# FFN's second product: one more slot of seven products, earlier first sums, and the last tile's end in column halves

## The chip, the core and the metric

The kernel runs on one core of a Trainium2 chip. The metric is the device time of one execution in microseconds (us). Five engines work side by side, each through its own instructions in order: TensorE (PE; its weight loads are PEld) multiplies, VectorE (DVE) and ScalarE (ACT) work on elements, GpSimd (POOL) does a few small things here, and SyncE (SP) issues nearly all DMA transfers.

## The reference

One decoder block for 256 tokens of width 2048 in float32: a retention branch and an attention branch, merged by gates, then a gated FFN of width 5632 with a causal convolution, and a final RMS norm. The change lies in the last lines of it:

```python
up = causal_dwconv(h2 @ w_ffn_up[l], conv_w[l], conv_b[l])
a, b = jnp.split(up, 2, axis=-1)
x = x + (jax.nn.silu(a) * b) @ w_ffn_down[l]
return rmsnorm(x, final_norm_w)
```

## The kernel before

**Products in three.** Each float32 operand is split into a first part (whi, gh, ...) and a second part, the rest (wlo, gl, ...), both of type fp32r. `split2` (line 158) makes them: ScalarE copies and rounds (line 161), VectorE subtracts (line 162). A product is three matmuls of 128x128 by 128x512, first by first, first by second, second by first (`mm3`, line 172).

**Weights.** All weights come as one stream of blocks of 128x1024. `load` brings a block into one of four `raw` buffers, `part` splits it into one of four pairs of part buffers, and when a block's splits are done, `part` issues the load of the block four places on. A slot uses two blocks. The loop of slot i issues first the splits for slot i+1, then the tasks that wait (`run_tasks`), then the matmuls of slot i; each engine's instructions keep this order.

**FFN.** The first product runs in groups of two 128-wide pieces ("up", four slots each, kc 0 to 3); its results g stay as 44 pieces, 22 blocks of two.

**The second product** (`down_slots`, line 794) is 2048 columns wide and taken in two pairs (p = 0, 1) of 512-wide columns. Each pair has 22 slots (q = 0 to 21). An ordinary slot multiplies a block of 256 rows by two columns for both token tiles: 8 products, 24 matmuls. A slot in `SEVEN` (line 82) does the same 2x2 scheme in seven products (21 matmuls), in the way of Strassen and Winograd. For it `seven_parts` (line 674) makes sums and differences of the weights, VectorE and ScalarE in turn, lines 680 to 695, in place of the two ordinary splits; and `seven_sums` (line 708) makes those of g once for each block, lines 714 to 718 and a split. The sums are used in both pairs: before, for blocks 0 to 5, made in loops q = 1, 4, 7, 10, 13 and 16 of the first pair.

**The end of the second pair.** After the last slot of seven, `gathered` (line 762) adds four extra accumulators into the residual in two halves of four VectorE operations (lines 770 to 773, 775 to 778), one in each of two loops. `added` adds the ordinary accumulators (line 783) and squares (line 787). `weighted` (line 789) multiplies by the final norm's weights wf. Slots 20 and 21 are held together: column 3 of their four blocks is computed for token tile 0 and then for tile 1, 24 matmuls each, and `finish` (line 530) ends each tile: add, squares, power on GpSimd (line 547), scale, store.

In the following, "slot n" without a pair is one of the second pair.

Of the kernel before, what the change touches and what calls it, by code (L numbers as in the profile page):

```python
# [9 lines left out]
F32 = mybir.dt.float32  # L10
# [68 lines left out]

SEVEN = ((4, 7, 10, 13, 16, 18), (3, 5, 8, 10, 13, 15))


def down():
# [16 lines left out]
def block(ctx: ExitStack, tc: tile.TileContext, a):  # L102
# [424 lines left out]
        yield  # L527
        split2(*ffn_slot(f), g)

    def finish(acc, t):  # L530

        c, half = D // CW - 1, CW // 2
        w = slice(c * CW, (c + 1) * CW)
        x3 = big["x2"][:, t, :]
        ms = sb.tile([P, 3], F32, name="r3ms", bufs=2)
        r = sb.tile([P, 1], F32, name="r3", bufs=2)
        nc.vector.reduce_sum(ms[:, 2:], big["ss3"][:, t, :c], axis=AX.X)  # L537
        nc.vector.tensor_scalar(ms[:, 0:1], ms[:, 2:], 1.0 / D, EPS, op0=OP.mult, op1=OP.add)  # L538
        pieces = [slice(c * CW + i * half, c * CW + (i + 1) * half) for i in range(2)]
        for i, v in enumerate(pieces):  # L540
            nc.vector.tensor_add(x3[:, v], acc[:, i * half:(i + 1) * half], x3[:, v])  # L541
        for i, v in enumerate(pieces):
            sq = sb.tile([P, half], F32, name="sq3", bufs=2)
            nc.scalar.activation(sq, x3[:, v], AF.Square, accum_out=big["ss3"][:, t, c + i:c + i + 1])  # L544
            nc.vector.scalar_tensor_tensor(ms[:, i + 1:i + 2], big["ss3"][:, t, c + i:c + i + 1], 1.0 / D,  # L545
                                           ms[:, i:i + 1], op0=OP.mult, op1=OP.add)
        nc.gpsimd.tensor_tensor(r, ms[:, 2:], mhalf[:, :1], op=OP.pow)  # L547
        nc.vector.tensor_mul(x3[:, w], x3[:, w], big["wf"][1][:, CW:])
        step = 448
        for b in range(0, 3 * step, step):  # L550
            w = slice(b, b + step)
            nc.vector.tensor_scalar_mul(x3[:, w], x3[:, w], r)  # L552
            nc.sync.dma_start(orows[:, t, w], x3[:, w])
        w = slice(3 * step, D)
        nc.scalar.activation(x3[:, w], x3[:, w], AF.Copy, scale=r)
        nc.scalar.dma_start(orows[:, t, w], x3[:, w])


    now = {}
# [145 lines left out]
            return ot[x + "h"][:, f % 8:f % 8 + 2, :], ot[x + "l"][:, f % 8:f % 8 + 2, :]  # L705
        return big["gh"][:, f - 16:f - 14, :], big["gl"][:, f - 16:f - 14, :]

    def seven_sums(k):


        ah, al = two_blocks(k)
        room = big["room"]
        x, sums = room[:, 0, :].rearrange("p (k t) -> p k t", k=2), room[:, 1, :].rearrange("p (i t) -> p i t", i=4)
        nc.vector.tensor_add(x, f32(ah), f32(al))
        nc.vector.tensor_add(sums[:, 0, :], x[:, 0, P:], x[:, 1, P:])
        nc.vector.tensor_sub(sums[:, 2, :], x[:, 0, :P], x[:, 0, P:])
        nc.vector.tensor_sub(sums[:, 1, :], sums[:, 0, :], x[:, 0, :P])
        nc.vector.tensor_sub(sums[:, 3, :], x[:, 1, :P], sums[:, 1, :])
        pool_k, tag = (px, f"xb{k}") if k < 5 else (big["pf"], "wa")
        big["s", k] = pool_k.tile([P, 2, 4, P], F32R, name=f"s{k}", tag=tag, bufs=1)  # L720
        split2(big["s", k][:, 0], big["s", k][:, 1], sums)

    def seven_products(k, accs, extra, halves):

        xs = two_blocks(k)
        sums = big["s", k]

        def a(t, kk):
            return [x[:, kk, t * P:(t + 1) * P] for x in xs]

        def b(half, kk):
            return [x[:, kk * CW:(kk + 1) * CW] for x in halves[half]]

        ss = [[sums[:, x, i, :] for x in range(2)] for i in range(4)]
        t1, t4 = [[x[:, i * CW:(i + 1) * CW] for x in big["t14"]] for i in range(2)]
        t2 = [big["t2"][:, x, :] for x in range(2)]
        for key, (ah, al), (bh, bl) in (
                ("e0", a(0, 0), b(0, 0)), ((0, 0), a(0, 1), b(0, 1)), ((0, 1), ss[3], b(1, 1)),
                ("e3", ss[2], b(1, 0)), ("e2", ss[1], t2), ("e1", ss[0], t1), ((1, 0), a(1, 1), t4)):
            begin, end = accs.edges(key, 3)  # L740
            mm3(accs.bank(key), ah, al, bh, bl, begin, end, to=stream)
# [52 lines left out]
    def down_slots(slot):  # L794
# [4 lines left out]
        for i, (seven, where) in enumerate(slots):  # L799
# [13 lines left out]
            if i + 1 < len(slots):  # L813
                if slots[i + 1][0]:
                    seven_parts(n)
                else:
                    part(n)
                    part(n + 1)
            if p == 0 and q in (1,) + SEVEN[0][:-1]:
                seven_sums(((1,) + SEVEN[0]).index(q))  # L820
            if q == SEVEN[p][-1] + 1:
                spawn(gathered, at)
            if p == 1 and q == SEVEN[1][-1] + 1:
                big["wf"] = [big["pf"].tile([P, 2 * CW], F32, name="wf", tag=x, bufs=1) for x in ("wa", "wb")]
                for j, wf in enumerate(big["wf"]):
                    nc.sync.dma_start(wf, a["wf"][None, 2 * CW * j:2 * CW * (j + 1)].to_broadcast([P, 2 * CW]))
            if p == 1 and q == per - 4:
                spawn(added, at.main[1], 3, False)
            if p == 1 and q == per - 3:
                weighted(0, 2)  # L830
            if p == 1 and q == per - 2:
                spawn(added, at.main[0], 2)
# [7 lines left out]
            elif p == 1 and q >= per - 2:  # L840
                if q == per - 2:
                    held = list(zip(where, halves))
                else:
                    held += zip(where, halves)
                    for t in range(NT):
                        acc = at.extra[t][:, 0, :]
                        for h, ((k, d), (hi, lo)) in enumerate(held):
                            for j in range(2):
                                x = [y[:, j, t * P:(t + 1) * P] for y in two_blocks(k)]
                                w = slice(j * CW, (j + 1) * CW)  # L850
                                mm3(acc, *x, hi[:, w], lo[:, w], h + j == 0, h == 3 and j == 1, to=stream)
                        issue()
                        finish(acc, t)
            else:
                for (k, d), (hi, lo) in zip(where, halves):
                    xs = two_blocks(k)
                    for j in range(2):
                        w = slice(j * CW, (j + 1) * CW)
                        for t in range(NT):
                            key = (t, d - 2 * p)  # L860
                            begin, end = at.edges(key, 3)
                            mm3(at.bank(key), *(x[:, j, t * P:(t + 1) * P] for x in xs), hi[:, w], lo[:, w],
                                begin, end, to=stream)
                issue()
# [29 lines left out]
    for kind, n, _, _, rows in groups:  # L894
# [10 lines left out]
        for kc in range(nk // 4):  # L905
            for h in range(2):
                part_x(4 * slot + 4 + 2 * h)
                part(2 * slot + 2 + h)
            run_tasks()
            halves = [parts.pop(2 * slot + h) for h in range(2)]  # L910
            products(kind, n, act, accs, kc, halves, range(NT), nk)
# [2 lines left out]
        closed(kind, n, acc, more)  # L914
    big["t14"] = [px.tile([P, 2 * CW], F32R, name=f"t14{i}", tag=f"xb{5 + i}", bufs=1) for i in range(2)]
    big["t2"] = px.tile([P, 2, CW], F32R, name="t2", tag="xb7", bufs=1)
    big["room"] = big["pf"].tile([P, 2, CW], F32, name="room", tag="wb", bufs=1)
    down_slots(slot)
    assert not tasks and not between
    right.close()  # L920
# [71 lines left out]
```

## Time and profile before

| what | us |
|---|---|
| median of three runs | 1432.77 (1432.64 to 1432.97) |
| the profiled execution | 1433.07 |
| its span, first to last instruction | 1431.3 |
| TensorE busy in the span | 1420.4 |
| VectorE busy | 977.1 |
| ScalarE busy | 743.4 |

The busy time of TensorE counts matmuls that overlap in its pipeline, so single matmuls last longer (0.39) than the distance of their starts. Times in rows are us from the first instruction.

### The profile page before, as it was taken

How to read it: one execution, taken by the hardware profiler on the slowest of the kernel's cores; microseconds unless marked ns; L12 is line 12 of the kernel's file. 1: busy time of each engine (PE TensorE's matmuls, PEld its weight loads, DVE VectorE, ACT ScalarE, POOL GpSimd, SP SyncE). 2: the span in 40 equal slices, each digit the busy share in tenths (PEclk: the TensorE clock that was granted, in tenths of full speed). 3: DMA queues.
4: the chain of work that ended last, by engine and by line, in shares of the span. 5: the costliest groups of instructions: out<-in, count | busy, mean ns of one | idle time of the engine just before them, and what ended most of it. 6: DMA issues, size and time to landing. Idle time of an engine off the chain costs nothing. (4 is left out here: it accounts for less than half of the span.)

```text
span 1431.3 us, 19149 instructions
## 1 busy us (share of the span) xinstructions
PE 1420.4 (99%) x7290; PEld 1214.8 (85%) x7290; DVE 977.1 (68%) x1296; ACT 743.4 (52%) x1006; POOL 6.0 (0%) x14
## 2 busy tenths in 40 slices
PE   9999999999999999999999999999999999999997
PEld 7888888888888888888888888888888888888886
DVE  6687656657554545455567777777777778898787
ACT  6545454544544444444465555555555555555553
POOL 0000000000000000000000000000000000000000
PEclk9999999999999999999999999999999999999999
DMA  8755565555566666666656666565665655656664
GB/s 295 263 181 163 163 190 167 189 175 189 180 186 196 187 195 186 195 214 200 195 188 189 194 182 197 182 195 188 188 194 181 199 181 168 198 192 206 206 215 167
DMA packets 77836, 276.22 MB, mean 193 GB/s; under 512 B 8720, under 2 KB 10288, under 8 KB 77744
## 3 DMA queue, kind: packets, MB, share of 16 engines
q1 hardware_dynamic: 77312, 274.27, 60.3%
q8 instruction: 57, 0.93, 0.3%
q10 hardware_dynamic: 432, 0.73, 0.1%
q14 instruction: 35, 0.29, 0.1%
HBM read 272.86 MB, written 2.10 MB: 192 GB/s over the span
## 5 line engine op out<-in xcount | busy, mean ns | idle before, releaser
L162 DVE TENSOR_TENSOR wlo<-raw,whi 128x1024 fp32r<-128x1024 f32 (+1 forms) x481 | 573.3, 1219 | 373.9 <-ACT whi L161 239.4
L161 ACT ACTIVATE whi<-raw 128x1024 fp32r<-128x1024 f32 (+1 forms) x481 | 502.2, 1056 | 513.7 <-PE acc L170 372.8
L170 PE MATMUL acc<-xb,whi 128*128 128x512 f32 x1920 | 466.2, 392 | 1.2 <-ACT whi L161 1.2
L170 PEld LDWEIGHTS acc<-xb,whi 128*128 128x128 f32 x1920 | 350.7, 188 | 68.8 <-ACT whi L161 2.3
L170 PE MATMUL acc<-whi,xb 128*128 128x512 f32 x896 | 282.1, 391 | 0.0
L170 PEld LDWEIGHTS acc<-xb,wlo 128*128 128x128 f32 x1920 | 250.8, 191 | 12.3
L170 PE MATMUL acc<-xb,wlo 128*128 128x256 f32 x1920 | 254.6, 282 | 0.0
L170 PEld LDWEIGHTS acc<-whi,xb 128*128 128x128 f32 x896 | 168.3, 188 | 34.4
L170 PE MATMUL acc<-wlo,xb 128*128 128x512 f32 x448 | 174.6, 390 | 0.0
L170 PEld LDWEIGHTS acc<-wlo,xb 128*128 128x128 f32 x448 | 84.2, 188 | 16.7
L170 PE MATMUL acc<-wlo,gh 128*128 128x512 f32 x224 | 87.4, 390 | 0.2 <-DVE wlo L162 0.2
L170 PE MATMUL acc<-whi,gl 128*128 128x512 f32 x224 | 87.2, 389 | 0.0
L170 PE MATMUL acc<-whi,gh 128*128 128x512 f32 x224 | 87.1, 389 | 0.0
L521 DVE SCALAR_TENSOR_TENSOR y<-u,vec,y 128x256 f32<-128x256 f32 x176 | 73.5, 480 | 0.0
L170 PEld LDWEIGHTS acc<-wlo,gh 128*128 128x128 f32 x224 | 42.0, 188 | 9.7 <-DVE wlo L162 1.0
L170 PE MATMUL acc<-whi,mgh 128*128 128x512 f32 x128 | 50.1, 392 | 0.0
L170 PE MATMUL acc<-whi,mgl 128*128 128x512 f32 x128 | 49.8, 389 | 0.0
L170 PE MATMUL acc<-wlo,mgh 128*128 128x512 f32 x128 | 49.8, 389 | 0.0
L170 PEld LDWEIGHTS acc<-whi,gh 128*128 128x128 f32 x224 | 42.0, 188 | 8.8
L170 PEld LDWEIGHTS acc<-whi,gl 128*128 128x128 f32 x224 | 42.0, 188 | 8.7
L518 ACT ACTIVATE y<-u,vec 128x256 f32<-128x256 f32 x88 | 47.6, 588 | 0.0
L170 PE MATMUL acc<-whi,otmh 128*128 128x512 f32 x104 | 40.6, 390 | 0.0
(206 smaller groups left out, 1167.9 us busy)
## 6 DMA issues: line engine op xcount, KB each, us to landing
raw<-in_wts SPq DMA_DIRECT2D x503, 512.0 KB, 4.0
rows<-in_x SPq DMA_DIRECT2D x4, 512.0 KB, 6.9
xp<-in_x SPq DMA_DIRECT2D x4, 512.0 KB, 5.2
xt<-in_xT SPq DMA_DIRECT2D x3, 512.0 KB, 7.2
out<-x SPq DMA_DIRECT2D x6, 224.0 KB, 2.9
wf<-in_wf SPq DMA_DIRECT2D x2, 512.0 KB, 7.2
out<-x ACTq DMA_DIRECT2D x2, 352.0 KB, 3.1
xt<-in_xT SPq DMA_DIRECT2D x2, 256.0 KB, 4.5
```

Of the source, the lines that this page charges most:

```text
L161: nc.scalar.activation(hi, full, AF.Copy)
L162: nc.vector.tensor_sub(lo, full, f32(hi))
L170: to.append(lambda: nc.tensor.matmul(out, a, b, **kw))
L518: nc.scalar.activation(y[:, j, :], u[:, j, 0:S], AF.Identity, scale=cv[j][:, 0:1], bias=cv[j][:, 3:4])
L521: nc.vector.scalar_tensor_tensor(y[:, j, :], u[:, j, i:i + S], cv[j][:, i:i + 1], y[:, j, :], op0=OP.mult, op1=OP.add)
```

## The change

- `SEVEN` gets a seventh slot in the second pair, 17; the sums of block 6 that it needs are made in loop 6 of that pair, into the room of two buffers of the FFN.
- The sums of block 0 are made in the FFN's last group (n = 42, kc = 1) and not in loop 1 of the first pair. They take the room where the sums of block 5 were, and those another.
- As `gathered` starts after the last slot of seven, its halves move from loops 16 and 17 to loops 18 and 19. The wf transfers are issued in loop 8 instead of 16, the first two columns are weighted in loop 11 instead of 19.
- The second token tile: its last block's products go into a second accumulator, in two halves of 256 columns; `finish` adds the first accumulator for the whole column and then half by half.
- `finish` writes the results in three transfers instead of four, 512, 1024 and 512 columns; the last column's multiplication by wf goes into its scaling.

```diff
--- before.py
+++ after.py
@@ -79,7 +79,7 @@
 
 
 
-SEVEN = ((4, 7, 10, 13, 16, 18), (3, 5, 8, 10, 13, 15))
+SEVEN = ((4, 7, 10, 13, 16, 18), (3, 5, 8, 10, 13, 15, 17))
 
 
 def down():
@@ -527,7 +527,7 @@
         yield
         split2(*ffn_slot(f), g)
 
-    def finish(acc, t):
+    def finish(acc, t, more):
 
         c, half = D // CW - 1, CW // 2
         w = slice(c * CW, (c + 1) * CW)
@@ -536,24 +536,30 @@
         r = sb.tile([P, 1], F32, name="r3", bufs=2)
         nc.vector.reduce_sum(ms[:, 2:], big["ss3"][:, t, :c], axis=AX.X)
         nc.vector.tensor_scalar(ms[:, 0:1], ms[:, 2:], 1.0 / D, EPS, op0=OP.mult, op1=OP.add)
+        if more is not None:
+            nc.vector.tensor_add(x3[:, w], acc, x3[:, w])
+            acc = more
         pieces = [slice(c * CW + i * half, c * CW + (i + 1) * half) for i in range(2)]
         for i, v in enumerate(pieces):
             nc.vector.tensor_add(x3[:, v], acc[:, i * half:(i + 1) * half], x3[:, v])
-        for i, v in enumerate(pieces):
             sq = sb.tile([P, half], F32, name="sq3", bufs=2)
             nc.scalar.activation(sq, x3[:, v], AF.Square, accum_out=big["ss3"][:, t, c + i:c + i + 1])
+        for i in range(2):
             nc.vector.scalar_tensor_tensor(ms[:, i + 1:i + 2], big["ss3"][:, t, c + i:c + i + 1], 1.0 / D,
                                            ms[:, i:i + 1], op0=OP.mult, op1=OP.add)
         nc.gpsimd.tensor_tensor(r, ms[:, 2:], mhalf[:, :1], op=OP.pow)
-        nc.vector.tensor_mul(x3[:, w], x3[:, w], big["wf"][1][:, CW:])
-        step = 448
-        for b in range(0, 3 * step, step):
+        step = CW
+        for b in range(0, D, step):
             w = slice(b, b + step)
-            nc.vector.tensor_scalar_mul(x3[:, w], x3[:, w], r)
-            nc.sync.dma_start(orows[:, t, w], x3[:, w])
-        w = slice(3 * step, D)
-        nc.scalar.activation(x3[:, w], x3[:, w], AF.Copy, scale=r)
-        nc.scalar.dma_start(orows[:, t, w], x3[:, w])
+            if b == step:
+                nc.scalar.activation(x3[:, b:b + 2 * step], x3[:, b:b + 2 * step], AF.Copy, scale=r)
+                nc.scalar.dma_start(orows[:, t, b:b + 2 * step], x3[:, b:b + 2 * step])
+            elif b == 0:
+                nc.vector.tensor_scalar_mul(x3[:, w], x3[:, w], r)
+                nc.sync.dma_start(orows[:, t, w], x3[:, w])
+            elif b == 3 * step:
+                nc.vector.scalar_tensor_tensor(x3[:, w], x3[:, w], r, big["wf"][1][:, CW:], op0=OP.mult, op1=OP.mult)
+                nc.sync.dma_start(orows[:, t, w], x3[:, w])
 
 
     now = {}
@@ -705,7 +711,7 @@
             return ot[x + "h"][:, f % 8:f % 8 + 2, :], ot[x + "l"][:, f % 8:f % 8 + 2, :]
         return big["gh"][:, f - 16:f - 14, :], big["gl"][:, f - 16:f - 14, :]
 
-    def seven_sums(k):
+    def seven_sums(k, pool_k, tag):
 
 
         ah, al = two_blocks(k)
@@ -716,9 +722,12 @@
         nc.vector.tensor_sub(sums[:, 2, :], x[:, 0, :P], x[:, 0, P:])
         nc.vector.tensor_sub(sums[:, 1, :], sums[:, 0, :], x[:, 0, :P])
         nc.vector.tensor_sub(sums[:, 3, :], x[:, 1, :P], sums[:, 1, :])
-        pool_k, tag = (px, f"xb{k}") if k < 5 else (big["pf"], "wa")
-        big["s", k] = pool_k.tile([P, 2, 4, P], F32R, name=f"s{k}", tag=tag, bufs=1)
-        split2(big["s", k][:, 0], big["s", k][:, 1], sums)
+        if isinstance(tag, str):
+            both = pool_k.tile([P, 2, 4, P], F32R, name=f"s{k}", tag=tag, bufs=1)
+            big["s", k] = both[:, 0], both[:, 1]
+        else:
+            big["s", k] = [pool_k.tile([P, 4, P], F32R, name=f"s{k}" + x, tag=x, bufs=1) for x in tag]
+        split2(*big["s", k], sums)
 
     def seven_products(k, accs, extra, halves):
 
@@ -731,7 +740,7 @@
         def b(half, kk):
             return [x[:, kk * CW:(kk + 1) * CW] for x in halves[half]]
 
-        ss = [[sums[:, x, i, :] for x in range(2)] for i in range(4)]
+        ss = [[x[:, i, :] for x in sums] for i in range(4)]
         t1, t4 = [[x[:, i * CW:(i + 1) * CW] for x in big["t14"]] for i in range(2)]
         t2 = [big["t2"][:, x, :] for x in range(2)]
         for key, (ah, al), (bh, bl) in (
@@ -816,17 +825,20 @@
                 else:
                     part(n)
                     part(n + 1)
-            if p == 0 and q in (1,) + SEVEN[0][:-1]:
-                seven_sums(((1,) + SEVEN[0]).index(q))
+            if p == 0 and q in SEVEN[0][:-1]:
+                k = SEVEN[0].index(q) + 1
+                seven_sums(k, px, f"xb{k % 5}")
+            if p == 1 and q == 6:
+                seven_sums(6, big["pf"], ("u0", "u1"))
             if q == SEVEN[p][-1] + 1:
                 spawn(gathered, at)
-            if p == 1 and q == SEVEN[1][-1] + 1:
+            if p == 1 and q == 8:
                 big["wf"] = [big["pf"].tile([P, 2 * CW], F32, name="wf", tag=x, bufs=1) for x in ("wa", "wb")]
                 for j, wf in enumerate(big["wf"]):
                     nc.sync.dma_start(wf, a["wf"][None, 2 * CW * j:2 * CW * (j + 1)].to_broadcast([P, 2 * CW]))
             if p == 1 and q == per - 4:
                 spawn(added, at.main[1], 3, False)
-            if p == 1 and q == per - 3:
+            if p == 1 and q == 11:
                 weighted(0, 2)
             if p == 1 and q == per - 2:
                 spawn(added, at.main[0], 2)
@@ -843,14 +855,20 @@
                 else:
                     held += zip(where, halves)
                     for t in range(NT):
-                        acc = at.extra[t][:, 0, :]
+                        acc, more = (at.extra[t][:, i, :] for i in range(2))
                         for h, ((k, d), (hi, lo)) in enumerate(held):
                             for j in range(2):
                                 x = [y[:, j, t * P:(t + 1) * P] for y in two_blocks(k)]
-                                w = slice(j * CW, (j + 1) * CW)
-                                mm3(acc, *x, hi[:, w], lo[:, w], h + j == 0, h == 3 and j == 1, to=stream)
+                                if t == 0 or h < 3:
+                                    w = slice(j * CW, (j + 1) * CW)
+                                    mm3(acc, *x, hi[:, w], lo[:, w], h + j == 0, h == 3 - t and j == 1, to=stream)
+                        for b in range(0, CW, CW // 2) if t else ():
+                            for j in range(2):
+                                x = [y[:, j, t * P:(t + 1) * P] for y in two_blocks(k)]
+                                w = slice(j * CW + b, j * CW + b + CW // 2)
+                                mm3(more[:, b:b + CW // 2], *x, hi[:, w], lo[:, w], j == 0, j == 1, to=stream)
                         issue()
-                        finish(acc, t)
+                        finish(acc, t, more if t else None)
             else:
                 for (k, d), (hi, lo) in zip(where, halves):
                     xs = two_blocks(k)
@@ -906,6 +924,9 @@
             for h in range(2):
                 part_x(4 * slot + 4 + 2 * h)
                 part(2 * slot + 2 + h)
+            if kind == "up" and n == NFB - 2 and kc == 1:
+                big["room"] = big["pf"].tile([P, 2, CW], F32, name="room", tag="wb", bufs=1)
+                seven_sums(0, big["pf"], "wa")
             run_tasks()
             halves = [parts.pop(2 * slot + h) for h in range(2)]
             products(kind, n, act, accs, kc, halves, range(NT), nk)
@@ -914,7 +935,6 @@
         closed(kind, n, acc, more)
     big["t14"] = [px.tile([P, 2 * CW], F32R, name=f"t14{i}", tag=f"xb{5 + i}", bufs=1) for i in range(2)]
     big["t2"] = px.tile([P, 2, CW], F32R, name="t2", tag="xb7", bufs=1)
-    big["room"] = big["pf"].tile([P, 2, CW], F32, name="room", tag="wb", bufs=1)
     down_slots(slot)
     assert not tasks and not between
     right.close()
```

## Rows read from the trace of the kernel before

**Rows 1.** Busy time by stage: stretch, length, engines PE, PEld, DVE, ACT, POOL, clock, DMA.
```profile
1168.20:1190.40 22.20, 22.20 (x130) 19.62 (x129) 16.48 (x25) 12.70 (x18) 0.00 (x0) 1.00 0.59 190
1342.80:1390.20 47.40, 47.40 (x211) 39.16 (x210) 39.32 (x47) 25.69 (x30) 0.00 (x0) 1.00 0.58 193
```

**Rows 2.** Waits of the DMA queue: who waited for whom, total us, times, longest.
```profile
SPq L144 <- DVE wlo L162: 1010.8, 372, 7.2
```

**Rows 3.** Timeline of TensorE, first pair: start, length, engine, line, operation, tiles, idle before.
```profile
1216.93 0.39 PE L170 MATMUL acc<-whi,gh 128*128 128x512 f32 x1
...
1222.69 0.39 PE L170 MATMUL acc<-whi,gh 128*128 128x512 f32 x1
1223.27 0.50 PE L170 MATMUL acc<-wlo,gh 128*128 128x512 f32 x1 [0.20 <-DVE wlo L162]
...
1228.66 0.39 PE L170 MATMUL acc<-whi,otrh 128*128 128x512 f32 x1
```

**Rows 4.** Timeline of VectorE, end of the first pair, then slots 7 to 15.
```profile
1279.07 0.68 DVE L714 TENSOR_TENSOR room<-otmh,otml 128x512 f32<-128x512 f32 x1
...
1282.45 1.23 DVE L684 TENSOR_TENSOR wlo<-raw,whi 128x1024 fp32r<-128x1024 f32 x1 [0.26 <-ACT whi L682]
...
1341.60 1.23 DVE L162 TENSOR_TENSOR wlo<-raw,whi 128x1024 fp32r<-128x1024 f32 x1 [0.78 <-ACT whi L161]
1343.78 1.22 DVE L684 TENSOR_TENSOR wlo<-raw,whi 128x1024 fp32r<-128x1024 f32 x1 [0.95 <-ACT whi L682]
...
1349.52 1.22 DVE L695 TENSOR_TENSOR t<-raw,t 128x1024 fp32r<-128x1024 f32 x1
...
1360.90 1.23 DVE L695 TENSOR_TENSOR t<-raw,t 128x1024 fp32r<-128x1024 f32 x1
...
1368.15 1.23 DVE L162 TENSOR_TENSOR wlo<-raw,whi 128x1024 fp32r<-128x1024 f32 x1 [1.27 <-ACT whi L161]
1369.42 1.23 DVE L684 TENSOR_TENSOR wlo<-raw,whi 128x1024 fp32r<-128x1024 f32 x1
...
1375.15 1.23 DVE L695 TENSOR_TENSOR t<-raw,t 128x1024 fp32r<-128x1024 f32 x1
...
1386.51 1.22 DVE L695 TENSOR_TENSOR t<-raw,t 128x1024 fp32r<-128x1024 f32 x1
```

**Rows 5.** Timeline of ScalarE, a step for slot 15.
```profile
1381.17 0.63 ACT L683 ACTIVATE whi<-raw 128x512 fp32r<-128x512 f32 x1 [1.07 <-DMA raw<-in_wts]
```

**Rows 6.** Timeline of TensorE: first matmul of slot 8, last matmul of all.
```profile
1349.29 0.39 PE L170 MATMUL acc<-whi,otrh 128*128 128x512 f32 x1
...
1422.61 0.39 PE L170 MATMUL acc<-whi,gl 128*128 128x512 f32 x1
```

**Rows 7.** Timeline of VectorE from loop 16 to the first tile's end.
```profile
1394.46 0.69 DVE L770 TENSOR_TENSOR x<-acc,x 128x512 f32<-128x512 f32 x1
...
1397.11 2.35 DVE L162 TENSOR_TENSOR wlo<-raw,whi 128x1024 fp32r<-128x1024 f32 x2
...
1408.95 2.28 DVE L792 TENSOR_TENSOR x<-x,wf 128x2048 f32<-128x2048 f32 x1
...
1414.39 1.22 DVE L783 TENSOR_TENSOR x<-acc,x 128x1024 f32<-128x1024 f32 x1
...
1418.54 0.75 DVE L541 TENSOR_TENSOR x<-acc,x 128x256 f32<-128x256 f32 x2
```

**Rows 8.** Timeline of the ends of both token tiles.
```profile
1420.17 0.55 POOL L547 TENSOR_TENSOR r<-r3ms,mhalf 128x1 f32<-128x1 f32 x1 [712.29 <-DVE r3ms L545]
...
1423.03 0.76 DVE L541 TENSOR_TENSOR x<-acc,x 128x256 f32<-128x256 f32 x2 [0.79 <-PE acc L170]
...
1424.51 0.68 DVE L548 TENSOR_TENSOR x<-x,wf 128x512 f32<-128x512 f32 x1
1424.67 0.93 POOL L547 TENSOR_TENSOR r<-r3ms,mhalf 128x1 f32<-128x1 f32 x1 [3.95 <-DVE r3ms L545]
```

**Rows 9.** Part 6 of the page, DMA issues: count, size, median us to landing.
```profile
wf<-in_wf SPq DMA_DIRECT2D x2, 512.0 KB, 7.2
```

## The prediction

> **What bounds the kernel now.** I read the stages first [rows 1]: between 1342.8 and 1390.2 us, in the second pair of the last product, TensorE is busy for all 47.4 us and VectorE for 39.3. TensorE sets the time as long as VectorE's operands are there early enough; the question for each edit is how early they are. Matmuls stand 0.227 us apart: from the first of slot 8 at 1349.29 to the last of all at 1422.61 are 323 steps [rows 6]. A slot of 24 is 5.44 us, a slot of seven products (21) is 4.76.
>
> **How early VectorE is.** The last step of `seven_parts` (line 695, the second parts of t1 and t4) is wanted by the 17th matmul of its slot, 16 steps or 3.63 us after the slot's start. Slots 8, 10, 13 and 15 start at 1349.29, 1359.49, 1375.13 and 1385.33 (the first row of [rows 6] and slots added to it). Line 695 ends at 1350.74, 1362.13, 1376.38 and 1387.73 [rows 4]. The leads are 2.18, 0.99, 2.38 and 1.23 us. A seven that comes two slots after another loses some 1.15: line 695 comes every 11.36 us there (1349.52 to 1360.90, 1375.15 to 1386.51) against 4.76 + 5.44 = 10.20 of TensorE. That rhythm isn't TensorE's: a load of weights waits until VectorE has done with the block two slots before [rows 2], and ScalarE, and VectorE after it, wait for its landing [rows 5]. So what delays VectorE in one seven delays the next as much. Three slots between sevens win the lead back.
>
> **First sums moved into the FFN.** Slots 5, 6 and 7 of the first pair start at 1216.93, 1222.69 and 1228.66 [rows 3]: 5.76 and 5.97 for slots of 5.44, so 0.32 + 0.53 = 0.85 us are lost, at the second matmul of each (0.58 instead of 0.23 in slot 6), which waits for a second part of the weights. The sums of block 0 stand ahead of these in VectorE's order. In the FFN's last group VectorE is busy for 16.5 of 22.2 us [rows 1], which covers the sums; uncovered they would cost their 3.4 (below) there. **-0.75**, with bounds of -0.85 and -0.5, since ScalarE's next part still waits for TensorE to free a buffer.
>
> **The seventh slot** saves 3 matmuls, 0.68 us of TensorE. It puts `seven_parts` (6.96 us from the start of line 684 to the end of 695, 1369.42 to 1376.38 [rows 4]) in the place of two splits (2.35, the merged row of [rows 7]): 4.6 us more of VectorE.
>
> **The sums for it, in loop 6,** stand behind slot 7's splits and ahead of `seven_parts` of slot 8. From line 714 to the next line 684 is 1279.07 to 1282.45 [rows 4], 3.38 us with ScalarE's step in it. Slot 7's second split lets the next operation start 1.14 after its own start (two take 2.35, one 1.22): 1341.60 + 1.14 + 3.38 = 1346.12 for slot 8's line 684, which came at 1343.78: **2.34 later**. The lead was 2.18; the stall is 0.3, with some 0.1 for the refill behind a wait (slot 6 of [rows 3] lost 0.53 for a wait of 0.35). Slot 10 is 2.34 later too and had 0.99: 1.2 more, refills included.
>
> **The weighting in loop 11** (2.28 long at 1408.95 in before [rows 7], the next one 2.2 behind its start) comes behind slot 12's second split, which hands over to slot 13's line 684 without a gap (1368.15, 1369.42 [rows 4]). That line comes at 1368.15 + 1.14 + 2.34 + 2.2 = 1373.83, **4.41 later**. TensorE is 1.5 late by then and the lead was 2.38: a stall of 0.53, with refills 0.7. Slot 15: 4.41 - 1.23 - 2.2 = 1.0, with refill 1.1. Slot 17: line 695 ends 11.36 after 1387.73 + 4.41 = 1392.14, at 1403.5; its slot starts at 1395.53 + 3.3 = 1398.8 and wants it at 1402.5: 1.1. TensorE is 4.4 late, and the 0.68 saved are paid several times over. The two wf transfers go out in loop 8 behind slot 11's loads (7.2 us to landing [rows 9]); they could hold up slot 12's loads, which are issued some 7 us later: 0, at most 2.
>
> **The end.** The sevens now end at slot 17, so `gathered` and column 3's `added` come in loops 18 and 19, where slots 19 and 20 are split, and not in 16 to 18. From the end of line 695 to the first operation of `gathered` lie the splits of two slots and their loads: 1387.73 to 1394.46, 6.73 us [rows 4, 7]. In VectorE's order follow, from 1403.5 + 6.73 = 1410.2: the first half of `gathered` 2.65 (1394.46 to 1397.11), line 783 for column 3 1.2, slot 20's splits 2.3, the second half 2.65, slot 21's splits 2.3, line 783 for column 2 1.2: 1422.5. TensorE starts the last two tiles at 1395.53 + 4.4 + 4.76 + 10.88 = 1415.6 and wants slot 21's first second part 13 steps on, at 1418.5; it is there at 1420.2. The stall is 1.8, TensorE's end some 1428.5. From the end of line 783 to the first tile's first add is 2.93 (1414.39 + 1.22 to 1418.54 [rows 7]): 1425.4. From there to the end of its power is 2.18 (1420.17 + 0.55 [rows 8]); two scalings of 512 columns 1.15 (estimate, at most 0.71 each by line 548), two tiny operations 0.3, the new whole-column add 0.7 (a quarter of 2.65). The second tile's first half is added at 1429.7, not at 1423.03 [rows 8]: **+6.7**. The twelve half-width matmuls lie between six full ones (as many columns) and twelve: 0 to 1.36 of TensorE, hidden either way, as VectorE is 1.2 behind TensorE's end and its second half's add 0.4 more.
>
> **Behind the last sum.** The second power took 0.93 us, the first 0.55; the second began 0.16 after the multiplication of line 548 and ended 0.41 after that one's end [rows 8]. That multiplication leaves this place: **-0.38**, bounds 0 and -0.5. The Trainium skill ("SBUF — State Buffer", Who interferes with whom) says that a VectorE tensor_tensor with both inputs in SBUF and a GpSimd operation that reads SBUF exclude each other, and that the one that starts first holds the other off to its end. By that rule the gain is due, without it the sum is 0.38 higher; the two rows agree with it. Each tile's 1 MB of results leaves in three transfers for four, the first one 64 columns wider: 0, estimated bounds -0.2 and +0.2.
>
> **Sum.** 6.7 - 0.38 - 0.75 = +5.6 on the profiled execution's 1433.07 (span 1431.3): 1438.6. The median of the runs shown lies 0.3 under the profiled one: **1438.3**, or +0.38%. A measurement of this kernel tells 0.2%, 2.9 us, from no change.
>
> **Rivals.** First, as meant: VectorE's added work is hidden. Then 3 matmuls, the first pair's stalls, the power and some 0.2 of the half-columns' overlap remain: -0.68 - 0.75 - 0.38 - 0.2 = -2.0, 1430.8. For it: 8 of VectorE's 47.4 us are idle [rows 1]. Against: those are waits for loads that are spent ahead of the added work in VectorE's order, and leads of 1 to 2.4 meet 2.34 and 2.2. Chance 0.10; half of it I give to a further gain that I don't see, under 1429.9.
> Second, the middle swallows sums and weighting (leads hold; slot 17's line 695 ends at 1399.1, wanted at 1399.16) and only the crowd of loops 18 to 20 is left. The end then lies 4.4 earlier: +6.7 - 4.4 - 0.38 - 0.75 = +1.2, 1433.9. It decides if slot 13's line 684 is late by under 1 us. Chance 0.14.
> Third, the wf transfers also hold up slot 12's and 13's loads, 2 us on the same chain: 1440.3. For it the 7.2 us to landing, against it that those loads are issued later. Chance 0.06.
> The forecast has 0.70, from 1436.3 to 1440 by its bounds: 0.25 for the first sums, 0.4 for the power, some 0.5 of landing time in each of three sevens, 0.3 for the first tile's scalings.
>
> **How the numbers follow.** The range, 1433.2 to 1440.5, holds the forecast and most of the second and third rivals. Slower by over 0.2% (above 1435.6): 0.72, nearly all of the forecast and part of the third. Within: the second, half of the first and the forecast's edge, 0.23. Faster: 0.05.
>
> **What would show it.** Right: slot 8's line 684 about 2.3 us later against its slot than in before, and slot 13's later still; TensorE waiting for lines 693 to 695 for about 1 us in slots 10, 13, 15 and 17, and for 1.8 in the last tile but one; VectorE almost without idle time from slot 8 on; the second tile's first add behind TensorE's end; a power of about 0.55. Wrong: TensorE without gaps in slots 8 to 17, or line 695 less than 1 us later against its slot.

## The result and the profile after

After the change a run takes 1441.22 us (median; 1440.52 to 1442.15), before it 1432.87 on the same chip (1432.64 to 1433.22): a ratio of 1.0058, interval 1.0041 to 1.0076. The change makes the kernel slower by 8.4 us. That is 2.9 over the forecast of 1438.3 and 0.7 over the upper end of the range. The profiled execution took 1441.75, before 1433.07: 8.68 more. The lines below are of it unless another kernel is named.

First, where TensorE waits: the waits of TensorE over the whole span (line, for whom, total us, times, longest).

```profile
PE acc L170 <- DVE x L787: 3.6, 1, 3.6
...
PE acc L170 <- DVE wlo L699: 1.7, 3, 0.9
...
PE acc L170 <- DVE t L701: 0.5, 3, 0.2
```

Lines 699 and 701 are the last second parts of `seven_parts` (line 695 before is now 701, and 684 now 690). The largest wait is another one: line 787 is the last operation of `gathered`, which stood in line 778 before.

How much each slot loses shows in the timeline of TensorE, as in [rows 3, 6]: from a slot's first matmul to the next slot's, less its 24 or 21 steps of 0.227. Before, slots 8 to 17 of the second pair lost 0.09 together.

| slot | 8 | 10 | 13 | 15 | 17 | sum | wait ahead of the last tile but one | lost in that tile |
|---|---|---|---|---|---|---|---|---|
| forecast | 0.3 | 1.2 | 0.7 | 1.1 | 1.1 | 4.4 | 0 | 1.8 |
| after | 0.22 | 1.18 | 0.37 | 1.70 | 1.22 | 4.69 | 3.75 | 1.72 |

VectorE in the stretch of [rows 4] (timeline: start, length, engine, line, operation, tiles, idle before):

```profile
1340.39 1.23 DVE L162 TENSOR_TENSOR wlo<-raw,whi 128x1024 fp32r<-128x1024 f32 x1 [0.83 <-ACT whi L161]
1341.53 0.68 DVE L720 TENSOR_TENSOR room<-otmh,otml 128x512 f32<-128x512 f32 x1
...
1344.92 1.22 DVE L690 TENSOR_TENSOR wlo<-raw,whi 128x1024 fp32r<-128x1024 f32 x1 [0.26 <-ACT whi L688]
...
1368.98 1.23 DVE L162 TENSOR_TENSOR wlo<-raw,whi 128x1024 fp32r<-128x1024 f32 x1 [1.04 <-ACT whi L161]
1370.12 2.29 DVE L801 TENSOR_TENSOR x<-x,wf 128x2048 f32<-128x2048 f32 x1
1372.32 1.22 DVE L690 TENSOR_TENSOR wlo<-raw,whi 128x1024 fp32r<-128x1024 f32 x1
```

Slot 8 starts at 1348.22, so line 690 leads it by 3.30; before, line 684 led by 1349.29 - 1343.78 = 5.51 [rows 4, 6]. It is 2.21 later against its slot. The weighting (line 801) puts another 2.2 ahead of slot 13's.

Then the end: TensorE from the last matmul of slot 19 on (timeline).

```profile
1414.62 0.39 PE L170 MATMUL acc<-whi,gl 128*128 128x512 f32 x1
1418.60 0.47 PE L170 MATMUL acc<-whi,gh 128*128 128x512 f32 x1 [3.59 <-DVE x L787]
...
1420.34 0.63 PE L170 MATMUL acc<-whi,gh 128*128 128x512 f32 x1
1420.77 0.63 PE L170 MATMUL acc<-wlo,gh 128*128 128x512 f32 x1
```

And VectorE in that time (timeline): the end of the first half of `gathered` (line 782), column 3's add (792), the end of the second half (787, the fourth of four operations without a pause), and column 2's add (792 again).

```profile
1411.58 0.69 DVE L782 TENSOR_TENSOR x<-acc,x 128x512 f32<-128x512 f32 x1
1412.30 1.23 DVE L792 TENSOR_TENSOR x<-acc,x 128x1024 f32<-128x1024 f32 x1
...
1417.76 0.69 DVE L787 TENSOR_TENSOR x<-acc,x 128x512 f32<-128x512 f32 x1
...
1420.63 1.22 DVE L792 TENSOR_TENSOR x<-acc,x 128x1024 f32<-128x1024 f32 x1
```

The windows of that stretch (start:end, length, busy time of PE, PEld, DVE, ACT and POOL with the instructions in brackets, granted clock, DMA share, GB/s):

```profile
1414.90:1418.60 3.70, 0.11 (x2) 0.03 (x1) 3.63 (x6) 1.06 (x1) 0.00 (x0) 1.00 0.00 0
...
1418.00:1420.00 2.00, 1.40 (x6) 1.15 (x7) 2.00 (x3) 0.00 (x0) 0.00 (x0) 0.93 0.05 12
1420.00:1422.00 2.00, 2.00 (x6) 1.57 (x5) 1.85 (x2) 0.11 (x1) 0.00 (x0) 0.50 0.00 0
1422.00:1424.00 2.00, 2.00 (x8) 1.59 (x7) 0.60 (x1) 1.33 (x4) 0.00 (x0) 0.72 0.00 0
```

TensorE stands still for 3.7 us while VectorE is busy, and behind that its granted clock falls from 1.00 (2.4 GHz) to 0.50 (1.2 GHz): matmuls come 0.43 us apart instead of 0.23, seven of them, with partly slow ones on either side; the tile loses 1.72 us in all. Last, the end of both tiles (timeline), against [rows 8]:

```profile
1431.15 0.28 PE L170 MATMUL acc<-whi,gl 128*128 128x256 f32 x1
1431.47 0.69 DVE L540 TENSOR_TENSOR x<-acc,x 128x512 f32<-128x512 f32 x1 [1.88 <-PE acc L170]
1432.19 0.76 DVE L544 TENSOR_TENSOR x<-acc,x 128x256 f32<-128x256 f32 x2
...
1433.83 0.55 POOL L550 TENSOR_TENSOR r<-r3ms,mhalf 128x1 f32<-128x1 f32 x1 [5.68 <-DVE r3ms L548]
```

The whole-column add of the first accumulator (line 540) was meant to run beside TensorE's last products. It waits until TensorE is done with everything.

**The account.** The 8.68 us of the profiled executions divide so, from the start to the end:

| where | forecast | measured |
|---|---|---|
| ahead of the first pair | 0 | -0.46 |
| first pair, slots 4 to 6 (4 loses 0.10 more, 5 and 6 lose 0.82 less) | -0.75 | -0.73 |
| other slots of both pairs (0.10 of it in slot 3 of the second) | 0 | +0.15 |
| three matmuls fewer | -0.68 | -0.68 |
| slots 8 to 17 | +4.4 | +4.62 |
| wait ahead of the last tile but one | 0 | +3.75 |
| lost in that tile | +1.8 | +1.72 |
| half-width matmuls, to the start of the last | 0 | +0.18 |
| from there to the second tile's first half added | +1.0 | +0.62 |
| power, with what leads to it | -0.38 | -0.38 |
| behind the power | 0 | -0.11 |
| sum | +5.4 | +8.68 |

The first row scatters: in the twelve runs below, whose front part is the same, it lies between -0.81 and +0.33, so it isn't put down to the change. The forecast's column is taken from its text; the 0.2 between its sum and the 5.6 there are roundings. The 3.1 that are missing come from the wait ahead of the last tile but one; and the 1.72 in that tile are no wait for slot 21's parts, as forecast, but nearly all the low clock.

### The profile page after: what moved, and what is told of

It is laid out like the page before. It is cut to its first block, busy times and chain, and to the rows that moved or that the text cites. A ratio compares the mean times of both kernels' runs of the same rounds, so it can differ in the third digit from the quotient of the medians.

```text
span 1440.0 us, 19163 instructions
## 1 busy us (share of the span) xinstructions
PE 1423.8 (99%) x7293; PEld 1215.6 (84%) x7293; DVE 983.7 (68%) x1306; ACT 745.8 (52%) x1010; POOL 5.6 (0%) x14
## 4 chain that ended last, share of the span: by engine, by line
PE 92%; DVE 4%; DMA 2%; issue 1%; ACT 1%; SPq 0%; DVEq 0%; POOLq 0%; POOL 0%; ACTq 0%
PE acc L170 90%; DMA raw<-in_wts 2%; DVE t L701 1%; PE ftr L178 0%; PE s L170 0%; PE rs L170 0%; PE o L170 0%; DVE raw L695 0%; DVE raw L693 0%; DVE raw L697 0%; DVE wlo L691 0%; PE ro L170 0%; DVE raw L692 0%; ACT whi L161 0%; DVE t L700 0%
## 5 line engine op out<-in xcount | busy, mean ns | idle before, releaser
L170 PE MATMUL acc<-whi,gh 128*128 128x512 f32 (+1 forms) x226 | 88.2, 390 | 3.6 <-DVE x L787 3.6
L170 PE MATMUL acc<-whi,gl 128*128 128x512 f32 (+1 forms) x226 | 88.2, 390 | 0.0
L170 PE MATMUL acc<-wlo,gh 128*128 128x512 f32 (+1 forms) x226 | 88.1, 390 | 0.0
```

The lines of the kernel that those rows point to most:

```text
L170: to.append(lambda: nc.tensor.matmul(out, a, b, **kw))
```

## The experiments

The theory: VectorE's added work in the middle and its crowding at the end make TensorE wait, as forecast; the end is worse than forecast because the accumulators stand in pairs of banks of which a whole pair is waited for, and because the standstill brings the clock down. Rivals for each part stand in the expectations. The kernels are all made from the changed one, but for the first-sums one. Each is given beside runs of the kernel before on its chip (1432.96, 1433.0 and 1433.2).

**The end: the pair of accumulators.** The kernel makes its accumulators as buffers of two banks of 512 columns each (a pair). In the last tile but one the kernel accumulates into `extra[0][:, 0]`. That bank is last read in the first half of `gathered`, which ended at 1412.3, 2.6 us before slot 19 did; line 787 reads `extra[0][:, 1]`, the other bank of the same pair. Two kernels give the tile a bank of another pair, `main[1]`, whose reader was done at 1413.5 (line 792, 1412.30 + 1.23); the second also lays the last tile's two accumulators into different pairs.

```diff
-acc, more = (at.extra[t][:, i, :] for i in range(2))
# e_bank
+acc, more = (at.main[1][:, 0, :], None) if t == 0 else (at.extra[1][:, 0, :], at.extra[1][:, 1, :])
# e_banks
+acc, more = (at.main[1][:, 0, :], None) if t == 0 else (at.extra[0][:, 0, :], at.extra[1][:, 0, :])
```

> The changed kernel, but the first token tile's last products go into the bank of column 3's ordinary accumulator, which VectorE has read by 1413.53 us in the trace of after, and not into the bank beside the one that the second half of gathered reads last (to 1418.45). Theory A (TensorE's 3.75 us ahead of the last tile but one is a wait for that pair of banks as a whole, and the slow clock behind it follows from the standstill): the wait goes, TensorE then waits some 1.8 us for slot 21's second parts, the clock stays at 1.00, and VectorE's own chain sets the end, 2.9 us earlier: 1438.3. Theory B (TensorE there waits for VectorE's backlog as such, the parts of slots 20 and 21): the wait only changes its name, and the time stays within 0.5 us of 1441.2.

Measured: 1440.88 us, ratio 1.0053 (1.0038 to 1.0068). The wait for line 787 is gone. In its place TensorE waits for slot 21's second parts, as it was forecast to for 1.8 us (waits of TensorE):

```profile
PE acc L170 <- DVE wlo L162: 1.9, 1, 1.9
```

Behind that wait of 1.87 the clock stays up (window, fields as above):

```profile
1422.00:1424.00 2.00, 1.49 (x6) 1.24 (x7) 2.00 (x3) 0.00 (x0) 0.00 (x0) 1.00 0.00 0
```

From slot 19's first matmul to the end of the second power it takes 22.03 us, against 24.97 in the changed kernel. But the time hardly fell, for this run lost 6.0 in slots 8 to 17 instead of 4.7, and the changed kernel had not run on this chip. So both were put on one chip, the changed kernel unaltered:

> The changed kernel once more, unaltered, as the yardstick for the three that run beside it on the same chip, since the loads' landing times differed between chips so far. Both theories: 1440 to 1442.5; slots 8 to 17 lose 4.5 to 6 us in all, the wait ahead of the last tile but one is 3.7 and the clock falls behind it.

Measured: 1441.04, ratio 1.0057 (1.0043 to 1.0071); the stretch takes 24.78 us, the slots lose 5.5.

> The changed kernel with the last products in three different pairs of banks: the first tile's in column 3's ordinary accumulators, the second tile's two in one pair each. Theory A (the wait for a pair of banks as a whole and the slow clock behind it cost 3 us at the end): from slot 19's first matmul to the end of the second power 22.0 us against 25.0 in the changed kernel, and a time 2.9 under the unaltered one beside it. Theory B (TensorE's wait there is hidden by VectorE's chain): no difference in time.

Measured: 1439.42, ratio 1.0042 (1.0029 to 1.0055), 1.62 under the unaltered one beside it; the stretch takes 21.92, 2.85 less. Slots 8 to 17 lost the same in both profiles (5.49 and 5.52). The timeline of the end:

```profile
1415.80 0.39 PE L170 MATMUL acc<-whi,gh 128*128 128x512 f32 x1
...
1418.74 0.69 DVE L787 TENSOR_TENSOR x<-acc,x 128x512 f32<-128x512 f32 x1
...
1420.62 0.50 PE L170 MATMUL acc<-wlo,gh 128*128 128x512 f32 x1 [1.71 <-DVE wlo L162]
...
1425.78 0.75 DVE L544 TENSOR_TENSOR x<-acc,x 128x256 f32<-128x256 f32 x2
...
1429.31 0.68 DVE L540 TENSOR_TENSOR x<-acc,x 128x512 f32<-128x512 f32 x1
1430.10 0.76 DVE L544 TENSOR_TENSOR x<-acc,x 128x256 f32<-128x256 f32 x2
...
1431.73 0.55 POOL L550 TENSOR_TENSOR r<-r3ms,mhalf 128x1 f32<-128x1 f32 x1 [3.78 <-DVE r3ms L548]
```

And the window behind the wait:

```profile
1422.00:1424.00 2.00, 2.00 (x11) 1.64 (x10) 0.84 (x1) 1.10 (x3) 0.00 (x0) 1.00 0.00 0
```

The last tile but one starts at 1415.80, without a wait and before line 787. In the changed kernel it waited for line 787, which reads the other bank only; so it was the pair, and not the bank, that was waited for. The Trainium skill ("PSUM — Partial Sum Buffer", Terms) says that two engines may not access the same bank at once; by that rule alone the tile's bank was free at 1412.3. The measured wait is longer than the rule asks for, by the kernel's own pairing. The clock stays at 1.00. In this kernel the end goes as it was forecast for the kernel: a stall of 1.71 (forecast 1.8), and from the end of column 2's add (line 792, 1421.62 + 1.22) to the second tile's first half 7.26 us (forecast 7.2), VectorE's chain being the limit. The profile's stretch became shorter by 2.85, the median by 1.6 and the mean of the five runs by 2.3; with five runs of each, which spread over 2.6 and 1.8 us, these don't contradict each other.

**The end: the clock.** In the changed kernel, 14 added matmuls into `main[1]` fill the standstill; their result goes unused, and nothing is left out.

```diff
 held += zip(where, halves)
+hi, lo = held[0][1]
+for _ in range(14):
+    mm(at.main[1][:, 0, :], two_blocks(held[0][0][0])[0][:, 0, :P], hi[:, :CW], start=True, stop=True, to=stream)
```

> The changed kernel with 14 more matmuls of 512 columns ahead of the last tile but one, into column 3's accumulator, whose result nobody reads: they take 14 x 0.227 = 3.2 us of the 3.75 in which TensorE stands still, and change no wait. Theory A (the 427 ns between matmuls behind the standstill are the lower clock, and the clock fell because TensorE did nothing): granted clock 1.00 throughout, the tile takes 5.4 us and not 7.16, the end comes 1.7 us earlier, 1439.5. Theory B (those matmuls were slow for another reason, such as operands that arrive late): no change, 1441.2.

Measured: 1441.22, ratio 1.0055 (1.004 to 1.007). The windows:

```profile
1418.00:1420.00 2.00, 1.53 (x7) 0.94 (x7) 1.97 (x3) 0.00 (x0) 0.00 (x0) 1.00 0.01 4
1420.00:1422.00 2.00, 2.00 (x10) 1.63 (x9) 2.00 (x3) 0.00 (x0) 0.00 (x0) 1.00 0.00 0
```

And what is left of the wait (waits of TensorE):

```profile
PE acc L170 <- DVE x L787: 0.5, 1, 0.5
```

Ten matmuls start in the stretch where the changed kernel started six, at a clock of 1.00. The stretch from slot 19 to the second power is 23.45, 1.5 less, near the 1.7 expected. The tile loses 0.13 instead of 1.72. So the clock's share is shown in the profile; the time, 1.7 over the one that theory A gave, is on the chip that had no run of the changed kernel, and doesn't tell.

**The middle.** Each of two kernels moves one piece of VectorE's work to a loop with more lead; a third makes both moves and has the banks of e_banks.

```diff
# e_sums5: the sums of block 6
-if p == 1 and q == 6:
+if p == 1 and q == 5:
# e_weigh17: the weighting of two columns
-if p == 1 and q == 11:
+if p == 1 and q == 17:
# e_all: both, and the line of e_banks
```

> The changed kernel with the sums of block 6 made in loop 5, behind slot 6's splits, and not in loop 6. Theory A (VectorE's order decides: in loop 5 the sums fall into the time in which VectorE waits for slot 7's loads, 1.28 + 0.83 us in the trace of after): line 690 of slot 8 comes 1.5 us earlier, slots 8 and 10 lose nothing or next to it, slot 13 and those behind keep 0.6 to 1.1 each; the time falls by 1.5 to 1439.7. Theory B (only the amount of VectorE's work counts, not its place): the stalls move but their sum of 4.7 us stays, 1441.2.

Measured: 1440.27, ratio 1.0049 (1.0032 to 1.0066), between the two. Slots 8, 10 and 13 lose nothing now (0.22, 1.18 and 0.37 in the changed kernel), slots 15 and 17 still 1.67 and 1.07. The gain of 2.0 is partly given back at the end, where the tile behind the standstill loses 2.58 instead of 1.72.

> The changed kernel with the first two columns weighted in loop 17, behind slot 18's splits, and not in loop 11. Theory A (place decides): there VectorE waits 1.34 + 0.93 us for slot 19's loads, so the 2.2 us cost next to nothing; slots 13 and 15 lose nothing, slot 17 about 1.0, and gathered starts 1.3 us earlier, which moves the end by as much: 1439.9. Theory B (only the amount of work counts): 1441.2, with the stalls of 13 and 15 found again at the end.

Measured: 1441.52, ratio 1.006 (1.0045 to 1.0075): no gain. Slot 13 loses nothing and slot 15 1.01 instead of 1.70. But slots 8 and 10, ahead of the edit, lose 1.28 and 1.62. One load of slot 7 landed 5.25 us after its issue here, and 4.39 in the changed kernel. In the six profiles with the sums in loop 6 slot 8's loss goes with that landing: landings of 4.39, 4.68, 4.74, 4.75, 4.97 and 5.25 stand beside losses of 0.21, 0.55, 0.51, 0.63, 0.90 and 1.28. The time can't judge the edit; the miss shows how a late landing goes into the time where no lead is left.

> The changed kernel with all three amendments: sums of block 6 in loop 5, weighting in loop 17, last products in three pairs of banks. Theory A: slots 8, 10 and 13 lose nothing, slots 15 and 17 together 1 to 2 us, the crowd of loops 18 to 20 still makes TensorE wait 1.5 in the last tile but one: 1435 to 1436, still slower than the kernel before, since the seventh slot's 4.6 us of VectorE's work don't fit in there. Theory B (only the order was wrong): the seventh slot's 0.68 and the 1.1 of the other parts come through, 1431.3.

Measured: 1435.62, ratio 1.0014 (1.0006 to 1.0023), as the theory has it; the rival, that the seventh slot then pays, is out. Slots 8 to 13 lose nothing, 15 and 17 0.48 and 0.80. The rest is in the end, where a wait and the clock are back (timeline of TensorE, then windows behind it):

```profile
1416.33 0.69 PE L170 MATMUL acc<-wlo,gh 128*128 128x512 f32 x1 [1.81 <-DVE wlo L162]
```

```profile
1417.00:1418.00 1.00, 1.00 (x4) 0.81 (x3) 1.00 (x2) 0.00 (x0) 0.00 (x0) 0.50 0.00 0
...
1417.00:1421.00 4.00, 4.00 (x14) 3.11 (x12) 2.46 (x3) 1.45 (x4) 0.00 (x0) 0.64 0.00 0
```

Here the clock fell to 0.50 behind a wait of 1.81, and the tile lost 3.69, the wait included. In e_banks it stayed at 1.00 behind 1.71, in e_bank behind 1.87.

**Without the seventh slot.** The next kernels undo the seventh slot and its sums, then also move the weighting back to loop 19, then also take the banks.

```diff
# e_no17
-SEVEN = ((4, 7, 10, 13, 16, 18), (3, 5, 8, 10, 13, 15, 17))
+SEVEN = ((4, 7, 10, 13, 16, 18), (3, 5, 8, 10, 13, 15))
-            if p == 1 and q == 6:
-                seven_sums(6, big["pf"], ("u0", "u1"))
# e_no17_w19: these, and
-            if p == 1 and q == 11:
+            if p == 1 and q == 19:
# e_best: these, and the line of e_banks
```

> The changed kernel without its seventh slot in the second pair (and without the sums for it): first sums in the FFN, early wf and weighting in loop 11, finish as changed. Theory A (VectorE's order decides): the weighting eats the leads of slots 13 and 15, slot 15 stalls by about 1.0; first pair -0.75, power -0.38; the second tile's first accumulator is added only when all of its pair of banks is done, +0.75: together +0.6, 1433.4. Theory B (the seventh slot is harmless and the rest costs): near 1441. Theory C (weighting in loop 11 is free): -0.4, 1432.4.

Measured: 1434.3, ratio 1.0007 (0.9998 to 1.0016). Without the seventh slot the loss falls from 0.58% to 0.07%. The time is 0.9 over theory A's, because slot 15 loses 2.02 and not 1.0 (waits of TensorE from 1340 to 1412 us):

```profile
PE acc L170 <- DVE wlo L699: 0.9, 1, 0.9
```

> As the one before, with the weighting back in loop 19. Theory A: no stall in slot 15 or another of the second pair, 1.0 less than with it in loop 11: 1432.4. If the weighting's place costs nothing, the two are equal.

Measured: 1432.76, ratio 0.9997 (0.9988 to 1.0005); no slot from 8 to 17 loses time. So the weighting in loop 11 costs 1.5 us by itself, by the medians of eleven runs each on one chip. In the profiles a part of the 2.02 can be the load for slot 15, which landed after 5.70 us in e_no17 and 4.99 here; but with the weighting in loop 19 a landing of 6.06 cost slot 15 only 0.46 (e_first, below), and one of 5.45 nothing (e_best, below).

> As the one before, and the second tile's two accumulators lie in two different pairs of banks, the first tile's in a third. Theory A (a reader waits for the last writer of the whole pair): the whole-column add runs beside TensorE's last twelve half-width matmuls, the first half's add still waits for the end of its bank, 0.7 less: 1431.7, faster than the kernel before by 1.1. Theory B (the wait is for the bank that is read, and the late add had another cause): equal to the one before.

Measured: 1432.07, ratio 0.9994 (0.9985 to 1.0003), the shortest of all, 0.93 under the kernel before, though the interval reaches 1. The last matmul and the last tile's first adds in e_no17_w19 (above) and in e_best (below), timelines of TensorE and VectorE:

```profile
1421.41 0.28 PE L170 MATMUL acc<-whi,gl 128*128 128x256 f32 x1
...
1421.73 0.69 DVE L540 TENSOR_TENSOR x<-acc,x 128x512 f32<-128x512 f32 x1 [0.94 <-PE acc L170]
1422.46 0.76 DVE L544 TENSOR_TENSOR x<-acc,x 128x256 f32<-128x256 f32 x2
```

```profile
1421.36 0.68 DVE L540 TENSOR_TENSOR x<-acc,x 128x512 f32<-128x512 f32 x1
...
1422.07 0.28 PE L170 MATMUL acc<-whi,gl 128*128 128x256 f32 x1
...
1422.38 0.76 DVE L544 TENSOR_TENSOR x<-acc,x 128x256 f32<-128x256 f32 x2 [0.34 <-PE acc L170]
```

The last matmuls start at 1421.41 and 1422.07. With both accumulators in one pair, line 540 comes behind the last matmul, and line 544 1.05 after it started; with different pairs line 540 runs beside TensorE, and line 544 comes after 0.31. The median is 0.69 lower. Even so the half columns gain nothing on the kernel before: from slot 19's first matmul to the end of the second power it takes 19.09 us there, 19.51 in e_no17_w19 and 18.78 in e_best, and the 0.31 less in e_best is no more than the 0.38 that the power gives. The first half's add never overlaps the second half's products, as it comes behind the last matmul in both kernels.

**The first sums alone,** in the kernel before:

```diff
-pool_k, tag = (px, f"xb{k}") if k < 5 else (big["pf"], "wa")
+pool_k, tag = (px, f"xb{k % 5}") if k else (big["pf"], "wa")
-if p == 0 and q in (1,) + SEVEN[0][:-1]:
-    seven_sums(((1,) + SEVEN[0]).index(q))
+if p == 0 and q in SEVEN[0][:-1]:
+    seven_sums(SEVEN[0].index(q) + 1)
+if kind == "up" and n == NFB - 2 and kc == 1:
+    big["room"] = big["pf"].tile([P, 2, CW], F32, name="room", tag="wb", bufs=1)
+    seven_sums(0)
-big["room"] = big["pf"].tile(...)   # stood behind the FFN
```

> The kernel before with one part of the change alone: the first block's sums made in the FFN's last group. Theory A: the first pair's slots 5 and 6 lose 0 to 0.1 and not 0.85, slot 4 may lose 0.1; -0.75, 1432.1. Theory B (the sums push the FFN's last group): TensorE waits there and nothing is gained.

Measured: 1432.21, ratio 0.9995 (0.9986 to 1.0003), 0.8 under the kernel before, as forecast (0.75); the interval reaches 1. In the profile slots 5 and 6 lose nothing and slot 4 loses 0.09.

**The power.** In e_best, a multiplication of 512 columns, whose product goes unused, stands ahead of the power, where line 548 before was.

```diff
+junk = big["pf"].tile([P, 2, S], F32, name="y", bufs=2).rearrange("p a t -> p (a t)")
+nc.vector.tensor_mul(junk, x3[:, :CW], big["wf"][1][:, CW:])
 nc.gpsimd.tensor_tensor(r, ms[:, 2:], mhalf[:, :1], op=OP.pow)
```

> The kernel without the seventh slot, with the weighting in loop 19 and three pairs of banks, and with one more VectorE multiplication of 512 columns (both inputs in SBUF, result unused) just ahead of the power. Theory A (such a multiplication that has begun holds the power up): the second power takes 0.9 again and not 0.55, 0.35 more in time. Theory B (the 0.93 in before was chance): 0.55, and no change, as VectorE has nothing else to do there.

Measured: 1432.31, ratio 0.9995 (0.9987 to 1.0004): the time doesn't tell it from e_best on another chip. The profile does: from slot 19's first matmul to the end of the second power it takes 19.18 us, 0.40 more than in e_best, where 0.35 was expected. The timeline:

```profile
1420.28 0.55 POOL L552 TENSOR_TENSOR r<-r3ms,mhalf 128x1 f32<-128x1 f32 x1 [713.21 <-DVE r3ms L548]
1420.30 0.71 DVE L551 TENSOR_TENSOR y<-x,wf 128x512 f32<-128x512 f32 x1
...
1424.69 0.68 DVE L551 TENSOR_TENSOR y<-x,wf 128x512 f32<-128x512 f32 x1
1424.86 0.93 POOL L552 TENSOR_TENSOR r<-r3ms,mhalf 128x1 f32<-128x1 f32 x1 [4.03 <-DVE r3ms L548]
```

Where the multiplication began 0.17 us before the power, the power takes 0.93; where it began 0.02 behind, the power takes 0.55. All kernels without the multiplication have 0.55 twice. By the rule of the Trainium skill ("SBUF — State Buffer", Who interferes with whom) that the forecast named, the operation that starts first holds the other off to its end. The trace agrees for the second power, which ended 0.42 after the multiplication. It doesn't agree for the first tile, where the power started first: the multiplication behind it took 0.71, hardly more than the 0.68 of the other one, and wasn't held off to the power's end.

## Why the prediction was right and wrong

- **What bounds the kernel, and how early VectorE is: right.** TensorE sets the time, and leads of 1 to 2.4 us were too small for additions of 2.3 and 2.2.
- **First sums: right,** -0.73 for -0.75. The FFN's last group covers them. The new losses of 0.10 in slot 4 of the first pair (within the -0.73) and in slot 3 of the second were not foreseen.
- **Sums in loop 6: right.** Line 690 of slot 8 is 2.21 later against its slot (forecast 2.34); slots 8 and 10 lose 0.22 and 1.18 (0.3 and 1.2). With the sums a loop earlier both losses are gone, as is slot 13's.
- **Weighting in loop 11: right in mechanism,** 2.2 us more ahead of slot 13. Slots 13, 15 and 17 lose 0.37, 1.70 and 1.22 for 0.7, 1.1 and 1.1. The 0.6 more in slot 15 are about what its load landed later (5.21 us after its issue for 4.66): in the six profiles with the seventh slot and the weighting in loop 11, slot 15's loss is that landing less 3.5, from 5.21 to 6.12. That the sum of the middle came out so near, 4.62 for 4.4, is in part luck: in e_again, the same kernel, slots 8 to 17 lost 5.5. The weighting costs 1.5 without the seventh slot beside it.
- **The seventh slot: right.** 0.68 saved, several times that lost. Without it the kernel is back within 0.07%.
- **VectorE's order at the end: right.** Column 2's add ends at 1421.85; 1422.5 was forecast, 1421.75 with the 0.75 of the first sums.
- **The end: this is the step that failed.** It let TensorE start the last two tiles without a wait and stall for 1.8 at slot 21's second parts. It looked at the weights alone and not at the accumulator: the tile's first matmul may not start before the second half of `gathered` has read the other bank of its pair. In the order that the text itself wrote out, that half ends 2.3 + 1.2 = 3.5 ahead of column 2's add, at 1419.0 on its clock, where TensorE's start stood at 1415.6: the 3.4 us stood in its own numbers, unasked for. Measured: 3.75. That wait comes first and swallows the 1.8. Taken away, the 1.71 appear.
- **Not in the sum at all: the clock.** A standstill was costed at its length; behind it seven to eight matmuls at 0.50 cost most of 1.72 more. The longer wait (3.75 - 1.8) and this are 3.7; the 0.46 ahead of the first pair and the 0.4 by which the last add came earlier behind TensorE take some of it back.
- **"Hidden either way": wrong.** The half columns' add can't run beside TensorE when both accumulators lie in one pair. As TensorE ended later than VectorE's work, it costs 0.7 behind the last matmul, where the forecast had VectorE 1.0 behind for another reason; the two nearly cancel.
- **Power: right,** -0.38, its reason shown. **Transfers:** the wf loads cost nothing visible, for e_no17_w19 issues them in loop 8 too and loses no time in slots 8 to 17; with the new result transfers it is -0.11 behind the power.

Open: why the load for slot 15 took 5.21 us to land (4.66 before). It isn't the change's alone: in e_first and e_mul, which have neither the seventh slot nor the weighting in loop 11, it took 6.06 and 6.65, and slot 15 lost 0.46 and 1.55. A transfer of instructions (16 KB, which took 0.9 to 2.1 us) runs during that load in all 14 profiles, the one of the kernel before included. It ends 2.45 to 4.43 us after the load's issue, and each time the load lands 1.9 to 2.3 us behind that end. So the two go together; as no kernel here moves that transfer by itself, it isn't shown that one delays the other.

## What to carry to other kernels

Before an operation that reads accumulators is moved later, list who writes next to the same buffer, in the unit in which the program waits (here a pair of banks), and set its end against that start; the weights' arrival is only one of TensorE's inputs. A product saved is worth its matmuls only where the engine that prepares it has lead to spare at that place: here 0.68 us was bought with 4.6 of VectorE. And a standstill of TensorE should be priced with a bound above its length, since the clock may be down behind it: here 1.5 to 2.6 us more for 3.6.

## What was not expected of the hardware

- With standstills of 3.55 to 3.65 us ahead of the last tile but one the granted clock fell from 1.00 to 0.50 (2.4 to 1.2 GHz) in all four profiles that had one, for 1.5 to 2.6 us of lost time. Behind 1.7 to 1.9 it stayed up twice (1.71, 1.87) and fell once (1.81, 3.69 lost with the wait). The length of the wait alone doesn't say which.
- The same kernel lost 0.21 us in slot 8 in one execution and 0.90 in another. Where no lead is left, the scatter of load landings (4.39 to 5.25 us for slot 7's) goes into the time. The load for slot 15 landed 1.9 to 2.3 us behind the end of a 16 KB transfer of instructions in all 14 profiles, after 4.66 to 6.65 us.
- A GpSimd operation on 128 single elements takes 0.55 us, and 0.93 when a VectorE multiplication with two inputs starts 0.17 us before it.
